# Squares for eight norms on ACT and their sums on DVE, in place of POOL, each behind the two parts of its tile

## The chip, the cores and the metric

The kernel runs on one core of one Trainium2 chip. The metric is device time in microseconds. The engines are named as the profile names them: PE (TensorE; PEld is its weight load), DVE (VectorE), ACT (ScalarE), POOL (GpSimd) and SP (SyncE, which issues nearly all transfers).

## What is computed

Two blocks in series on 256 tokens of width 1024, all in fp32. The first block has two layers: a gated feed-forward half step, then a state-space mixer (mamba) in layer 0 or a sliding-window attention in layer 1, then a second half step. The second block is a mixer of two parts (latent attention and a recurrence) and a retrieval feed-forward ("peer") of 16,384 experts. Each stage begins with a root-mean-square norm of the residual:

```python
def rmsnorm(x, g):
    xf = x.astype(jnp.float32)
    y = xf * lax.rsqrt(jnp.mean(xf * xf, axis=-1, keepdims=True) + EPS)
    return (y * g.astype(jnp.float32)).astype(x.dtype)

def swiglu_half_step(h, g, w1, w3, w2):
    u = rmsnorm(h, g)
    return h + FFN_HALF * ((jax.nn.silu(u @ w1) * (u @ w3)) @ w2)
```

There are eight such norms: one at the head of each of the four half steps, of the mamba mixer, of the attention, of the second block's mixer and of the peer stage.

## The kernel before

The residual `h` stays in on-chip memory, features on the partitions: eight tiles of 128 features by 256 tokens, `h[:, 0]` to `h[:, 7]`. Every fp32 product is made of three reduced-precision ones: an operand is split into a high part (rounded) and a low part (the rest), and `mm3` (lines 151 to 155) multiplies low by high, high by low and high by high into one sum. Weights come in chunks of eight blocks of 128 by 128 (`stream`, line 102): SP loads a chunk (`wraw`, four buffers), ACT rounds it (`whi`, line 93), DVE takes the difference (`wlo`, line 99); in the mixers some chunks have POOL take the difference.

The norm's factor is one number per token, so it is applied behind the first projection of a stage. What a stage needs first of the residual is therefore two things:

- The parts of `h` times the norm's gain. `split_x` (line 178) makes them tile by tile: ACT writes `xhi` (line 181), DVE writes `xlo` (line 182), which waits for it. In the peer stage they are called `uhi` and `ulo`.
- The sum of squares over the features. `norm_sum` (line 200) gives one tile's share at each step: on POOL a square (line 206 for tile 0, line 209 for the others, two buffers `sq`), and for tiles 1 to 7 an addition into `ssq` (line 210). `rs_tok` (line 184) then sums over the partitions with four small matmuls against ones (line 190), and DVE makes the reciprocal root in nine small steps (lines 168 to 176, tiles `qna`, `qny`, `qnt`, `rtn`). These matmuls stand behind the first one or two pairs of projections.

`norm_in` (line 213) runs both for seven norms: in each turn of its loop first the square and sum of tile k, then its split. The peer stage has the same loop written out, with the same order of square and split.

In a half step's second product the tiles of `h` come ready one after the other (line 319), some 8 us apart. Behind the mamba mixer (line 509), the attention and the second mixer (both line 261) they come in pairs: one addition of 512 columns finishes two tiles.

The program is written in one order, and a scheduler lays the instructions out on each engine's queue. On an engine they run strictly in that order.

Of the kernel before, what the change touches and what calls it, by code (L numbers as in the profile page):

```python
# [12 lines left out]
AF = mybir.ActivationFunctionType  # L13
# [5 lines left out]
KD = 8  # L19
# [29 lines left out]
class Ctx:  # L49
# [150 lines left out]
    def norm_sum(self, h):  # L200

        nc = self.nc
        acc = self.tmp.tile([128, T], F32, name="ssq", tag="ssq")
        for k in range(KD):
            if k == 0:
                nc.gpsimd.tensor_mul(acc, h[:, k], h[:, k])
            else:
                s = self.tmp.tile([128, T], F32, name="sq", tag="sq", bufs=2)
                nc.gpsimd.tensor_mul(s, h[:, k], h[:, k])
                nc.gpsimd.tensor_add(acc, acc, s)  # L210
            yield acc

    def norm_in(self, h, g):

        nc = self.nc
        hi = self.xp.tile([128, KD, T], F32R, name="xhi", tag="xhi")
        lo = self.xp.tile([128, KD, T], F32R, name="xlo", tag="xlo")
        for k, acc in enumerate(self.norm_sum(h)):
            self.split_x(h, g, hi, lo, k)

        def scale(between=None, tok=False):
            rt = self.rs_tok(acc, self.ones[:, 0:1], 1, 1.0 / 1024, EPS, "n")
            if tok:
                return rt
            if between is not None:
                between()
            ps = self.bank()
            for st in range(2):
                self.bcast(rt, st, 0, 128, ps[:, st * 128:(st + 1) * 128])
            rs = self.tmp.tile([128, T], F32, name="rs", tag="rs", bufs=2)  # L230
            nc.scalar.activation(rs, ps[:, :T], AF.Copy)
            return rs, rt

        return hi, lo, scale
# [1735 lines left out]
```

## Time and profile before

| what | us |
|---|---|
| three timed runs: lowest, median, highest | 2182.05, 2186.6, 2188.41 |
| profiled execution, its own time | 2188.62 |
| its span (first to last instruction) | 2186.8 |
| PE busy, share of the span | 2109.8, 96% |
| PEld busy | 1986.3, 91% |
| DVE busy | 1584.8, 72% |
| ACT busy | 1055.1, 48% |
| POOL busy | 407.1, 19% |

Busy matmul time is an upper bound of what PE needs, as matmuls overlap and their ends are modelled. What PE loses is to be read from its idle stretches and from the clock that it was granted, place by place. The mean granted clock of the profiled execution was 0.973 of full speed.

### The profile page before, as it was taken

The numbers are of one execution on the slowest core, as the hardware profiler recorded it, in microseconds if no ns is written. First come the engines' busy times: TensorE is split into PE (matmuls) and PEld (weight loads), VectorE is DVE, ScalarE is ACT, GpSimd is POOL, SyncE is SP. The second block draws the span as 40 slices with busy tenths as digits, with TensorE's granted clock in tenths as the row PEclk, the third lists the DMA queues.
The fourth block names the chain that finished last, engine by engine and source line by source line (L and its number), as shares of the span: only waits on it lengthen the run. The fifth ranks groups of instructions, "written<-read, shape, count | busy, mean of one in ns | idle before, by whom it ended". The sixth has DMA issues, their size and how long they took to land. (4 is left out here: it accounts for less than half of the span.)

```text
span 2186.8 us, 40880 instructions
## 1 busy us (share of the span) xinstructions
PE 2109.8 (96%) x16474; PEld 1986.3 (91%) x16474; DVE 1584.8 (72%) x2857; ACT 1055.1 (48%) x1770; POOL 407.1 (19%) x310
## 2 busy tenths in 40 slices
PE   8999898899999999999998998999999999999999
PEld 8999887799999998899997878999999998888887
DVE  7665979766567656676659678998788887555655
ACT  5444467444444445454443345553444444454454
POOL 2003335700110021100144315762000000000000
PEclk9999999999999999799998899999999999999999
DMA  6555442377555553245542205542444444555554
GB/s 218 190 185 177 136 135 101 134 191 204 185 181 184 183 184 107 102 169 188 188 164 76 80 30 194 177 151 97 157 162 155 159 160 164 189 188 191 192 188 150
DMA packets 98280, 348.14 MB, mean 159 GB/s; under 512 B 11083, under 2 KB 13996, under 8 KB 97836
## 3 DMA queue, kind: packets, MB, share of 16 engines
q1 hardware_dynamic: 98092, 345.54, 46.6%
q8 instruction: 129, 2.11, 0.4%
q14 instruction: 59, 0.48, 0.1%
HBM read 344.05 MB, written 1.44 MB: 158 GB/s over the span
## 5 line engine op out<-in xcount | busy, mean ns | idle before, releaser
L99 DVE TENSOR_TENSOR wlo<-wraw,whi 128x1024 fp32r<-128x1024 f32 x561 | 701.7, 1252 | 293.9 <-ACT whi L93 292.0
L93 ACT ACTIVATE whi<-wraw 128x1024 fp32r<-128x1024 f32 x644 | 676.5, 1053 | 394.0 <-PE ps L155 198.8
L153 PE MATMUL ps<-xhi,wlo 128*128 128x256 f32 x1960 | 562.7, 287 | 20.4 <-DVE wlo L99 9.6
L154 PE MATMUL ps<-xlo,whi 128*128 128x256 f32 x1960 | 557.3, 284 | 3.2 <-DVE xlo L182 2.6
L155 PE MATMUL ps<-xhi,whi 128*128 128x256 f32 x1960 | 554.9, 283 | 0.0
L153 PEld LDWEIGHTS ps<-xhi,wlo 128*128 128x128 f32 x1960 | 376.2, 192 | 28.8 <-DVE wlo L99 8.6
L154 PEld LDWEIGHTS ps<-xlo,whi 128*128 128x128 f32 x1960 | 376.1, 192 | 5.8 <-DVE xlo L182 5.4
L155 PEld LDWEIGHTS ps<-xhi,whi 128*128 128x128 f32 x1960 | 375.5, 192 | 0.2
L153 PE MATMUL ps<-phi,wlo 128*128 128x256 f32 x1024 | 293.9, 288 | 11.3 <-DVE wlo L99 4.6
L154 PE MATMUL ps<-plo,whi 128*128 128x256 f32 x1024 | 288.1, 281 | 0.0
L155 PE MATMUL ps<-phi,whi 128*128 128x256 f32 x1024 | 287.2, 281 | 0.0
L99 POOL TENSOR_TENSOR wlo<-wraw,whi 128x1024 fp32r<-128x1024 f32 (+1 forms) x83 | 206.8, 2495 | 167.5 <-ACT whi L93 145.5
L153 PEld LDWEIGHTS ps<-phi,wlo 128*128 128x128 f32 x1024 | 193.8, 190 | 13.1 <-DVE wlo L99 5.3
L1676 PE MATMUL pacc<-whi,cl 128*128 128x512 f32 x512 | 203.6, 398 | 1.5 <-DVE cl L1668 1.5
L1678 PE MATMUL pacc<-whi,ch 128*128 128x512 f32 x512 | 200.5, 392 | 0.0
L1677 PE MATMUL pacc<-wlo,ch 128*128 128x512 f32 x512 | 199.2, 389 | 0.0
L153 PE MATMUL ps<-ghi,wlo 128*128 128x256 f32 x704 | 197.9, 281 | 0.0
L154 PE MATMUL ps<-glo,whi 128*128 128x256 f32 x704 | 197.6, 281 | 0.0
L155 PE MATMUL ps<-ghi,whi 128*128 128x256 f32 x704 | 197.5, 280 | 0.0
L154 PEld LDWEIGHTS ps<-plo,whi 128*128 128x128 f32 x1024 | 194.0, 189 | 0.0
L155 PEld LDWEIGHTS ps<-phi,whi 128*128 128x128 f32 x1024 | 193.3, 189 | 0.0
L154 PEld LDWEIGHTS ps<-glo,whi 128*128 128x128 f32 x704 | 132.6, 188 | 0.0
(534 smaller groups left out, 3371.3 us busy)
## 6 DMA issues: line engine op xcount, KB each, us to landing
wraw<-in_w SPq DMA_DIRECT2D x262, 512.0 KB, 3.7
wraw<-in_p_u SPq DMA_DIRECT2D x128, 512.0 KB, 3.6
wraw<-in_p_v SPq DMA_DIRECT2D x128, 512.0 KB, 3.6
wraw<-in_m_win SPq DMA_DIRECT2D x40, 512.0 KB, 3.7
wraw<-in_x_win SPq DMA_DIRECT2D x20, 512.0 KB, 3.6
wraw<-in_m_wout SPq DMA_DIRECT2D x16, 512.0 KB, 3.7
wraw<-in_p_wpq SPq DMA_DIRECT2D x16, 512.0 KB, 4.3
wraw<-in_a_wq SPq DMA_DIRECT2D x8, 512.0 KB, 3.5
```

The costliest lines, as they stand in the source:

```text
L93: nc.scalar.activation(hi, w, AF.Copy)
L99: (nc.vector if lo_eng == "dve" else nc.gpsimd).tensor_sub(lo, w, hi.bitcast(F32))
L153: nc.tensor.matmul(ps, wl, xh, start=first, stop=False)
L154: nc.tensor.matmul(ps, wh, xl, start=False, stop=False)
L155: nc.tensor.matmul(ps, wh, xh, start=False, stop=last)
L1676: TE.matmul(o, cl[:, t], vh[:, f], start=False, stop=False)
L1677: TE.matmul(o, ch[:, t], vl[:, f], start=False, stop=False)
L1678: TE.matmul(o, ch[:, t], vh[:, f], start=False, stop=last)
```

## The change

```diff
--- before.py
+++ after.py
@@ -203,11 +203,11 @@
         acc = self.tmp.tile([128, T], F32, name="ssq", tag="ssq")
         for k in range(KD):
             if k == 0:
-                nc.gpsimd.tensor_mul(acc, h[:, k], h[:, k])
+                nc.scalar.activation(acc, h[:, k], AF.Square)
             else:
                 s = self.tmp.tile([128, T], F32, name="sq", tag="sq", bufs=2)
-                nc.gpsimd.tensor_mul(s, h[:, k], h[:, k])
-                nc.gpsimd.tensor_add(acc, acc, s)
+                nc.scalar.activation(s, h[:, k], AF.Square)
+                nc.vector.tensor_add(acc, acc, s)
             yield acc
 
     def norm_in(self, h, g):
@@ -215,8 +215,10 @@
         nc = self.nc
         hi = self.xp.tile([128, KD, T], F32R, name="xhi", tag="xhi")
         lo = self.xp.tile([128, KD, T], F32R, name="xlo", tag="xlo")
-        for k, acc in enumerate(self.norm_sum(h)):
+        sums = self.norm_sum(h)
+        for k in range(KD):
             self.split_x(h, g, hi, lo, k)
+            acc = next(sums)
 
         def scale(between=None, tok=False):
             rt = self.rs_tok(acc, self.ones[:, 0:1], 1, 1.0 / 1024, EPS, "n")
```

The square of a tile is taken by ACT and the addition by DVE. In `norm_in` the split of tile k now stands ahead of its square and sum; in the peer stage the square and sum still stand ahead of the split in the program's order. Lines behind 219 move by two: line 261 before is line 263 now.

How the queues change is shown at three places. The first is DVE behind the attention, at the last two pairs of tiles: `h<-h,ps` finishes a pair, `xlo` is the low part, `wlo` a chunk of the next half step's weights. Before:

```order
L99 TENSOR_TENSOR wlo<-wraw,whi 128x1024
L182 SCALAR_TENSOR_TENSOR xlo<-h,gains,xhi 128x256 x2
L261 TENSOR_TENSOR h<-h,ps 128x512
L99 TENSOR_TENSOR wlo<-wraw,whi 128x1024
L182 SCALAR_TENSOR_TENSOR xlo<-h,gains,xhi 128x256 x2
L99 TENSOR_TENSOR wlo<-wraw,whi 128x1024 x3
```

Now:

```order
L210 TENSOR_TENSOR ssq<-ssq,sq 128x256
L99 TENSOR_TENSOR wlo<-wraw,whi 128x1024
L182 SCALAR_TENSOR_TENSOR xlo<-h,gains,xhi 128x256
L263 TENSOR_TENSOR h<-h,ps 128x512
L210 TENSOR_TENSOR ssq<-ssq,sq 128x256
L182 SCALAR_TENSOR_TENSOR xlo<-h,gains,xhi 128x256
L210 TENSOR_TENSOR ssq<-ssq,sq 128x256
L182 SCALAR_TENSOR_TENSOR xlo<-h,gains,xhi 128x256
L210 TENSOR_TENSOR ssq<-ssq,sq 128x256
L182 SCALAR_TENSOR_TENSOR xlo<-h,gains,xhi 128x256
L210 TENSOR_TENSOR ssq<-ssq,sq 128x256
L99 TENSOR_TENSOR wlo<-wraw,whi 128x1024 x4
```

Each low part has an addition behind it, the pair's addition into `h` stands among them, and one `wlo` that stood ahead of the last two low parts stands behind them.

The second place is ACT at the very start; `whi` of 128x512 is half a chunk. Before:

```order
L181 ACTIVATE xhi<-h,gains 128x256 x2
L123 ACTIVATE whi<-wraw 128x512
L181 ACTIVATE xhi<-h,gains 128x256 x2
L123 ACTIVATE whi<-wraw 128x512
L181 ACTIVATE xhi<-h,gains 128x256 x4
L123 ACTIVATE whi<-wraw 128x512 x2
L93 ACTIVATE whi<-wraw 128x1024 x7
```

Now:

```order
L181 ACTIVATE xhi<-h,gains 128x256
L206 ACTIVATE ssq<-h 128x256
L181 ACTIVATE xhi<-h,gains 128x256
L123 ACTIVATE whi<-wraw 128x512
L209 ACTIVATE sq<-h 128x256
L181 ACTIVATE xhi<-h,gains 128x256
L209 ACTIVATE sq<-h 128x256
L123 ACTIVATE whi<-wraw 128x512
L181 ACTIVATE xhi<-h,gains 128x256
L209 ACTIVATE sq<-h 128x256
L181 ACTIVATE xhi<-h,gains 128x256
L209 ACTIVATE sq<-h 128x256
```

Squares stand between the high parts, and seven of the eight stand ahead of the last high part.

The third place is ACT at the peer stage's norm; `bhi` belongs to the mixer, `pq` to the peer's first product. Before:

```order
L1417 ACTIVATE ahi<-ps,px 128x128 x8
L93 ACTIVATE whi<-wraw 128x1024 x2
L1187 ACTIVATE bhi<-ps 128x4x128
L93 ACTIVATE whi<-wraw 128x1024 x5
L181 ACTIVATE uhi<-h,pa 128x256 x8
L93 ACTIVATE whi<-wraw 128x1024
L1542 ACTIVATE pq<-ps 128x256
```

Now:

```order
L206 ACTIVATE ssq<-h 128x256
L209 ACTIVATE sq<-h 128x256
L93 ACTIVATE whi<-wraw 128x1024
L209 ACTIVATE sq<-h 128x256 x2
L93 ACTIVATE whi<-wraw 128x1024
L209 ACTIVATE sq<-h 128x256 x2
L181 ACTIVATE uhi<-h,pa 128x256 x6
L209 ACTIVATE sq<-h 128x256
L181 ACTIVATE uhi<-h,pa 128x256
L209 ACTIVATE sq<-h 128x256
L181 ACTIVATE uhi<-h,pa 128x256
L93 ACTIVATE whi<-wraw 128x1024
```

Six squares stand ahead of all high parts, beside the chunks that still belong to the mixer's last product; two stand ahead of the last two high parts.

On PE the order changes at five places by a few matmuls. At two of them, behind mamba and behind the attention, four matmuls that before stood among the first projection's, with a later weight chunk, now stand behind it. At the attention's norm the four small matmuls on `ssq` move behind the first projection. On POOL the 120 instructions of lines 206, 209 and 210 go, and no other is added.

## Rows read from the trace of the kernel before

**Rows 1.** The page, part 1: busy time, share of the span, instructions.

```profile
PE 2109.8 (96%) x16474; PEld 1986.3 (91%) x16474; DVE 1584.8 (72%) x2857; ACT 1055.1 (48%) x1770; POOL 407.1 (19%) x310
```

**Rows 2.** Groups by line, POOL: count | busy us, mean ns | idle before.

```profile
L210 POOL TENSOR_TENSOR ssq<-ssq,sq 128x256 f32<-128x256 f32 x56 | 58.5, 1045 | 3.3
L209 POOL TENSOR_TENSOR sq<-h 128x256 f32<-128x256 f32 x56 | 52.2, 939 | 159.6 <-DVE h L319 152.3 <-DVE nsink L657 5.5 <-DVE h L261 1.0
```

**Rows 3.** Line 182 by itself: min/median/max ns, first and last start.

```profile
L182 DVE SCALAR_TENSOR_TENSOR xlo<-h,gains,xhi x56: 472/831/2620, 4.8 to 1120.5; 128x256 fp32r<-128x256 f32 x56
L182 DVE SCALAR_TENSOR_TENSOR kvlo<-h,gains,kvhi x8: 472/475/476, 629.3 to 633.2; 128x256 fp32r<-128x256 f32 x8
```

**Rows 4.** Groups by line, DVE and ACT: busy us, mean ns of 128x256 operations.

```profile
L289 DVE TENSOR_TENSOR glo<-fab,ghi 128x256 fp32r<-128x256 f32 x88 | 37.2, 424 | 31.8 <-ACT ghi L288 31.8
L182 DVE SCALAR_TENSOR_TENSOR ulo<-h,pa,uhi 128x256 fp32r<-128x256 f32 x8 | 6.1, 832 | 0.0
L286 ACT ACTIVATE fab<-fab 128x256 f32<-128x256 f32 x88 | 35.4, 402 | 9.5 <-DVE fab L284 9.5
```

**Rows 5.** Timeline, DVE, attention to the next block: start us, us, what.

```profile
919.23 1.37 DVE L99 TENSOR_TENSOR wlo<-wraw,whi 128x1024 fp32r<-128x1024 f32 x1 [0.40 <-ACT whi L93]
...
928.76 0.68 DVE L261 TENSOR_TENSOR h<-h,ps 128x512 f32<-128x512 f32 x1
...
931.00 1.70 DVE L182 SCALAR_TENSOR_TENSOR xlo<-h,gains,xhi 128x256 fp32r<-128x256 f32 x2
```

**Rows 6.** Timeline, POOL, the same place.

```profile
929.28 2.39 POOL L210 TENSOR_TENSOR ssq<-ssq,sq 128x256 f32<-128x256 f32 x2
```

**Rows 7.** Timeline, PE, the same place.

```profile
926.36 0.28 PE L155 MATMUL ps<-ohi,whi 128*128 128x256 f32 x1
...
930.03 0.38 PE L153 MATMUL ps<-xhi,wlo 128*128 128x256 f32 x1 [0.64 <-ACT xhi L181]
```

**Rows 8.** Busy time by stretch: PE, PEld, DVE, ACT, POOL (x), PEclk, DMA, GB/s.

```profile
13.80:22.60 8.80, 8.78 (x73) 8.67 (x74) 7.36 (x7) 3.18 (x3) 6.63 (x5) 1.00 0.66 216
933.00:943.00 10.00, 10.00 (x75) 10.00 (x74) 3.68 (x3) 3.35 (x4) 1.59 (x3) 0.83 0.48 165
```

**Rows 9.** Timeline, DVE, mixer (mamba) to the next block.

```profile
425.62 3.30 DVE L182 SCALAR_TENSOR_TENSOR xlo<-h,gains,xhi 128x256 fp32r<-128x256 f32 x2 [0.86 <-ACT xhi L181]
...
429.44 1.21 DVE L99 TENSOR_TENSOR wlo<-wraw,whi 128x1024 fp32r<-128x1024 f32 x1
...
435.44 0.68 DVE L509 TENSOR_TENSOR h<-h,wo 128x512 f32<-128x512 f32 x1
...
437.74 1.70 DVE L182 SCALAR_TENSOR_TENSOR xlo<-h,gains,xhi 128x256 fp32r<-128x256 f32 x2
```

**Rows 10.** Timeline, POOL, the same place.

```profile
426.04 2.59 POOL L99 TENSOR_TENSOR wlo<-wraw,whi 128x1024 fp32r<-128x1024 f32 x1
```

**Rows 11.** Timeline, DVE, last block to the router (peer).

```profile
1335.78 6.11 DVE L182 SCALAR_TENSOR_TENSOR ulo<-h,pa,uhi 128x256 fp32r<-128x256 f32 x8
```

**Rows 12.** Timeline, PE, first waiting matmul at four other norms.

```profile
203.29 0.31 PE L154 MATMUL ps<-xlo,whi 128*32 128x256 f32 x1 [0.72 <-DVE xlo L182]
...
629.45 0.39 PE L154 MATMUL ps<-xlo,whi 128*128 128x256 f32 x1 [0.38 <-DVE xlo L182]
...
829.08 0.61 PE L190 MATMUL ps<-ones,ssq 128*128 128x1 f32 x4 [0.41 <-POOL ssq L210]
...
1125.25 0.61 PE L190 MATMUL ps<-ones,ssq 128*128 128x1 f32 x4 [0.61 <-POOL ssq L210]
```

**Rows 13.** Timeline, ACT, the first microseconds.

```profile
7.90 0.63 ACT L123 ACTIVATE whi<-wraw 128x512 fp32r<-128x512 f32 x1 [0.98 <-DMA wraw<-in_w]
8.57 1.71 ACT L181 ACTIVATE xhi<-h,gains 128x256 fp32r<-128x256 f32 x4
```

**Rows 14.** Timeline, DVE, the first microseconds.

```profile
9.42 3.33 DVE L182 SCALAR_TENSOR_TENSOR xlo<-h,gains,xhi 128x256 fp32r<-128x256 f32 x4
```

**Rows 15.** Timeline, PE, the first microseconds.

```profile
13.82 0.38 PE L153 MATMUL ps<-xhi,wlo 128*128 128x256 f32 x1 [0.52 <-DVE wlo L124]
```

## The prediction

> **What bounds the kernel now.** I read the page first: PE is busy for 96% of the span [rows 1], so the work of the norms can only matter where PE waits for it. The two views that say where are the timeline of PE around each of the eight norms, and the timelines of DVE and POOL beside it. POOL is not the bound, and the 110.7 us that lines 209 and 210 take of it [rows 2] are not on PE's path as such. The question is what these POOL instructions do to DVE.
>
> A low part (line 182) lasts 472 to 475 ns where POOL is empty, which is the case for the eight `kvlo`, and in the median 831 ns beside POOL's squares [rows 3]. The longest took 2.62 us, and the pair that holds it ran 425.62 to 428.92 while POOL had a weight chunk from 426.04 to 428.63 [rows 9, 10]. So a DVE instruction with two tensors from on-chip memory waits until POOL's instruction ends, and the reverse: two POOL additions took 2.39 us beside a DVE chunk [rows 6], 1.2 us each, close to their mean of 1.05 us [rows 2]. The Trainium skill says the same of this pair of engines (SBUF — State Buffer, Who interferes with whom): whichever starts first holds a shared port for its whole instruction. The trace agrees, with the numbers above.
>
> This matters where DVE is behind. Behind the attention PE ended the last matmul of the residual at 926.64 [rows 7], but DVE added that pair into `h` only at 928.76, and ended the last low part at 932.70 [rows 5]. PE stood still in between [rows 7], and from 933 on it was granted 0.83 of full speed [rows 8]. Behind mamba the last low part ended at 439.44 [rows 9].
>
> **The change, part by part.** POOL loses 120 instructions, and its queue keeps only weight chunks near the norms. ACT gets 64 squares and DVE 56 additions. No row shows a square of this kind. The nearest is an activation of 128x256 from and to on-chip memory, 402 ns; the nearest to the addition is `glo`, 424 ns [rows 4]. DVE starts an instruction before the last one has ended: eight `ulo` of 832 ns fill 6.11 us, not 6.66 [rows 4, 11], an overlap of 0.08 us. ACT's high parts follow each other at 0.43 us (four in 1.71 us) [rows 13]. So from start to start I take 0.34 us for an addition, 0.40 for a low part alone, 0.40 for a square, 1.13 for a chunk (1.21) [rows 9] and 0.60 for a pair's addition into `h` (0.68) [rows 5].
>
> *The middle tiles of the half steps* come some 8 us apart and meet a DVE and an ACT that wait for PE there; 0.34 and 0.40 us per tile cost nothing. If that cover were gone, the first to be late would be a weight chunk, with buffers for three ahead.
>
> *Four norms at which one tile is last.* PE waited 0.72 us (mamba) and 0.38 us (third half step) for the last low part, and 0.41 us (attention) and 0.61 us (second mixer) for POOL's sum [rows 12]. Alone the low part is 0.36 us shorter, and the chunk ahead of it at mamba isn't stretched either: I take 0.6 and 0.35 us back. At the second mixer the sum is on DVE, ahead of a chunk: 0.6 us. At the attention PE's order now has the low part first, which is just late: 0.2 us. Together 1.75 us (between 1.2 and the whole 2.1).
>
> *Behind the attention.* From 919.23 [rows 5] DVE has, up to the last low part, three chunks instead of four (the order shows the fourth behind), eight low parts, three pairs, and six additions: 3.4 + 3.2 + 1.8 + 2.0 = 10.4 us. With some 0.4 us of waits for ACT the last low part ends at 930.0 instead of 932.70. PE had used 0.5 us of its wait for four matmuls of a later sum, which it can't any more. That leaves 2.2 us. The ends are 1.5 us, if ACT's squares delay the high parts, and 3.8 us, if the lower clock behind it goes as well.
>
> *Behind mamba.* The first two low parts wait for POOL's chunk as before. From 429.44 [rows 9] on there are two chunks instead of three ahead of the last low part, six low parts, two pairs, and five additions: 2.3 + 2.4 + 1.2 + 1.7 = 7.6 us, which gives 437.05 instead of 439.44. Six matmuls that PE then did early (0.12 us each: 73 in 8.78 us [rows 8]) come off: 1.6 us (between 1.0 and 3.2, as above). If POOL merely slowed DVE, as the median of 831 against 475 ns could also be read, the first two low parts would not block, and it would be 2.7 us. By the skill's rule of the held port they do block; with it the whole sum is 6.3 us, without it 7.4. I go by the rows of the blocked pair, which are the nearer ones [rows 9, 10].
>
> *The peer stage.* Eight low parts follow each other, 6.11 us [rows 11]; now eight at 0.40 and two additions, 3.9 us: 2.2 us (between 1.5 and 2.6, for two squares of 0.40 us ahead of the last high parts, and for the chunks ahead of them that POOL no longer stretches).
>
> *The very start costs.* DVE was slowed here too (four low parts in 3.33 us [rows 14]), but ACT now has seven squares ahead of the last high part, and DVE additions between the low parts. From 7.90, where ACT gets the second half chunk [rows 13], it has five high parts, three half chunks and four squares up to the last high part: 2.1 + 1.6 + 1.6 = 5.3 us, so 13.2, where all high parts were done at 10.28 [rows 13]. The last low part then ends near 14.2, and the second half of the first projection starts near 14.45 instead of 13.82 [rows 15]: +0.6 us. PE also idles more in these microseconds. If it is then at the lower of its two levels, 1.2 instead of 2.4 GHz, those 24 matmuls cost another 24 x 0.12 = 2.9 us. I take +1.5, between +0.6 and +3.5, nearer to the lower end, since the clock is free to rise within them.
>
> **The sum.** +1.5 - 1.75 - 2.2 - 1.6 - 2.2 = -6.25, so 6.3 us less. Against the profiled execution's 2188.62 that is 2182.3. That execution lies 2.0 us above the median of the runs, 2186.6; the forecast for the median is **2180.3 us**. With all bounds at one end the gain is 11.1 us (2175.5), at the other 1.7 us (2184.9).
>
> **Rivals.** *The clock comes back.* Behind the attention PE lost 0.17 of 10 us to the lower level [rows 8]. With shorter waits both this stretch and the like one behind mamba may stay at the higher level: 3.2 us more, 2177.1. For it: the waits there shrink by half. Against it: PE still waits for low parts five to seven, one by one.
>
> *The start stays slow.* PE runs the whole second half of its first projection at the lower level: 3.5 instead of 1.5 us lost, 2182.3. For it: PE will have long gaps between 8 and 14 us. Against it: before, it was also idle in part there, and ran at full speed by 13.8 [rows 8]. The Trainium skill has a rule for this (TensorE: Matmul & The Clock Gate, What's actually happening): the slow level is the default, and activity releases it. By that rule this rival is what would happen, as the gaps now lie where the activity was; the granted clock at the start is what will tell.
>
> *Slower.* POOL is not what lengthens the low parts, so they stay at 0.83 us, and every addition is work put in front: seven at the start (2.4 us), five behind mamba (1.7), six behind the attention (2.0), two and two squares at the peer stage (1.5), less 0.8 us of waits for POOL's sum: 6.8 us more, 2193.4. The place is the DVE queue behind the attention. It decides by one duration: a low part and its addition together have to stay under the 0.83 us of a low part now, so the low part alone under 0.83 - 0.34 = 0.49 us; above that the queue is longer than before. Against it: `kvlo` on the same engine between the same neighbours at 475 ns [rows 3].
>
> **How the numbers follow.** I give the forecast 0.55, the clock's return 0.17, the slow start 0.22, and the slower case 0.06. A difference of 0.3%, about what a measurement can tell here, is 6.6 us, and the forecast's 6.3 lies almost on it: of its 0.55 I count 0.26 as over and 0.29 as within. So faster by over 0.3% is 0.26 + 0.17 = 0.43; within it 0.29 + 0.22 = 0.51; slower 0.06. The first three cases with their bounds reach from 2175.5 to 2184.9; the runs before lie up to 4.5 us from their median, so I take 1.5 us more below and 2.6 above. The range, 2174.0 to 2187.5, leaves out the last case.
>
> **What would show it.** In the changed profile the median of line 182 should be near 475 ns, with the longest still over 2 us behind mamba. Behind the attention the last low part should end about 2.7 us sooner after the same matmul, and behind mamba 2.4. The four small waits should be gone or under 0.2 us. At the start the second half of the first projection should begin 0.6 us later, and the granted clock there tells the first two cases of the start apart. Squares should take 0.40 us and additions 0.42. The forecast is wrong if low parts stay over 0.7 us, if a chunk on ACT is late because of squares in front of it during the half steps' second products, or if the total differs although these places move as said; then a place that I take to be unchanged has moved.

## The result and the profile after

The changed kernel takes 2175.54 us in the median of 18 runs (2163.42 to 2179.73), the kernel before 2185.41 in the median of 18 (2173.3 to 2195.81). The ratio is **0.9947, 95% interval 0.9929 to 0.9965**: 0.53% faster (0.35 to 0.71), in microseconds 0.0053 x 2185.4 = 11.6 (7.7 to 15.5). The two medians lie 9.9 us apart. The forecast was 6.3 us, and the likeliest single outcome in it was a difference within 0.3%. The time lies in the range that was given, 1.5 us above its lower end. The profiled execution took 2176.04 us, 12.6 less than that of before.

On the page of the changed kernel POOL's share falls (19% before, [rows 1]), and PE's rises by one point, which is the smaller span:

```profile
PE 2105.8 (97%) x16474; PEld 1983.6 (91%) x16474; DVE 1581.8 (73%) x2913; ACT 1074.8 (49%) x1834; POOL 292.8 (13%) x190
```

DVE has 56 instructions more and is busy for 3 us less. Line 182 by itself says why (min/median/max ns; compare [rows 3]):

```profile
L182 DVE SCALAR_TENSOR_TENSOR xlo<-h,gains,xhi x56: 470/479/2334, 4.9 to 1112.9; 128x256 fp32r<-128x256 f32 x56
L182 DVE SCALAR_TENSOR_TENSOR kvlo<-h,gains,kvhi x8: 477/479/481, 629.4 to 633.4; 128x256 fp32r<-128x256 f32 x8
L182 DVE SCALAR_TENSOR_TENSOR ulo<-h,pa,uhi x8: 475/476/478, 1325.4 to 1328.8; 128x256 fp32r<-128x256 f32 x8
```

The median went from 831 to 479 ns, the value that `kvlo` always had. The longest is still 2.33 us. Squares and additions cost what the nearest rows said (groups by line, ACT and DVE: busy us, mean ns):

```profile
L209 ACT ACTIVATE sq<-h 128x256 f32<-128x256 f32 x56 | 22.3, 402 | 0.5 <-DVE ssq L210 0.4
L210 DVE TENSOR_TENSOR ssq<-ssq,sq 128x256 f32<-128x256 f32 x56 | 23.4, 418 | 0.2
```

Behind the attention (timeline of DVE, the changed kernel; compare [rows 5]), the last low part now ends at 926.35, which is 11.6 us after the first of these `h` additions has begun at 914.75:

```profile
914.75 0.69 DVE L263 TENSOR_TENSOR h<-h,ps 128x512 f32<-128x512 f32 x1 [0.52 <-PE ps L155]
...
923.47 0.68 DVE L263 TENSOR_TENSOR h<-h,ps 128x512 f32<-128x512 f32 x1
...
925.87 0.48 DVE L182 SCALAR_TENSOR_TENSOR xlo<-h,gains,xhi 128x256 fp32r<-128x256 f32 x1
926.26 0.42 DVE L210 TENSOR_TENSOR ssq<-ssq,sq 128x256 f32<-128x256 f32 x1
```

In the kernel before, the additions at the same places began at 424.07 behind mamba and at 918.14 behind the attention (timeline of DVE):

```profile
424.07 0.69 DVE L509 TENSOR_TENSOR h<-h,wo 128x512 f32<-128x512 f32 x1 [7.64 <-PE wo L155]
...
918.14 0.69 DVE L261 TENSOR_TENSOR h<-h,ps 128x512 f32<-128x512 f32 x1 [0.67 <-PE ps L155]
```

The last low part behind the attention ended at 932.70, 14.6 us later. So DVE is 3.0 us sooner here (2.7 was forecast). Behind mamba (compare [rows 9]) the same distance is now 439.94 + 0.47 - 427.69 = 12.7 us, where it was 439.44 - 424.07 = 15.4: 2.7 us sooner (2.4 forecast).

```profile
427.69 0.69 DVE L511 TENSOR_TENSOR h<-h,wo 128x512 f32<-128x512 f32 x1 [7.67 <-PE wo L155]
429.23 2.73 DVE L182 SCALAR_TENSOR_TENSOR xlo<-h,gains,xhi 128x256 fp32r<-128x256 f32 x2 [0.85 <-ACT xhi L181]
...
439.94 0.47 DVE L182 SCALAR_TENSOR_TENSOR xlo<-h,gains,xhi 128x256 fp32r<-128x256 f32 x1
```

The pair of 2.73 us is the one that still meets a weight chunk on POOL, as forecast. What the forecast had only as a rival stands in the next rows: the ten microseconds behind both last low parts (busy time by stretch; after the POOL column PEclk, DMA share, GB/s), where [rows 8] had a granted clock of 0.83 behind the attention, and where the first row here, of the kernel before, has 0.91 behind mamba; the two below it are the changed kernel's:

```profile
439.50:449.50 10.00, 10.00 (x80) 10.00 (x80) 3.92 (x5) 3.80 (x4) 1.82 (x3) 0.91 0.47 147
```

```profile
440.50:450.50 10.00, 10.00 (x88) 10.00 (x89) 5.95 (x12) 4.24 (x4) 0.00 (x0) 1.00 0.67 194
926.40:936.40 10.00, 10.00 (x87) 10.00 (x88) 5.89 (x9) 4.24 (x4) 0.00 (x0) 1.00 0.57 179
```

PE now runs at its full clock through both.

What PE waited for just before these stretches in the kernel before were low parts, and weight chunks (`wlo`) in the same DVE queue (timeline of PE, behind mamba and then behind the attention):

```profile
434.82 0.39 PE L154 MATMUL ps<-xlo,whi 128*128 128x256 f32 x1 [1.08 <-DVE xlo L182]
...
437.97 0.55 PE L153 MATMUL ps<-xhi,wlo 128*128 128x256 f32 x1 [0.88 <-DVE wlo L99]
...
931.23 0.36 PE L153 MATMUL ps<-xhi,wlo 128*128 128x256 f32 x1 [0.81 <-DVE wlo L99]
```

At each of the two places there was a wait for a high part besides (0.63 us, and 0.64 in [rows 7]). These two places, behind mamba and behind the attention, are called the handovers from here on.

**Where the time went, place by place.** Each matmul of one program has its like in the other (same source line, same operands, same count). The table takes the difference of their start times, in the median over a stretch behind a place less the median over a stretch ahead of it. All columns are against the first profile of the kernel before; `again` and `third` are further executions of the same two kernels, described below. The first eight rows are the places of the eight norms, in the order of the program; negative is sooner.

```
us                      before  before   after   after   after
                        again   third    first   again   third
start of the program      2.25    1.37    2.56    1.89    2.36
mamba's norm             -0.01    0.00   -0.66   -0.66   -0.66
behind mamba              0.09   -0.01   -3.33   -2.74   -2.99
third half step           0.00    0.00   -0.48   -0.48   -0.49
attention's norm         -0.01    0.00   -0.20   -0.20   -0.20
behind the attention      0.01    0.24   -4.35   -3.57   -4.35
second mixer's norm       0.00    0.01   -0.88   -0.88   -0.88
peer stage's norm         0.01    0.14   -2.30   -1.97   -1.99
inside mamba              1.95    1.15    1.71    2.35    1.66
inside the attention      0.06    0.02   -2.99   -0.01   -2.99
inside the second mixer  -4.41   -4.02   -1.95   -3.93   -1.68
```

The seven norms behind the start repeat to within 0.8 us, four of them to 0.01. They sum to -12.2, -10.5 and -11.6 us, -11.4 in the mean, which is the size of the measured 11.6. The start, the first row, is taken up below. Inside the mixers the *same* program differs by several us between executions.

### The profile page after: what moved, and what is told of

It is laid out like the page before. It is cut to its first block, busy times and chain, and to the rows that moved or that the text cites. A ratio compares the mean times of both kernels' runs of the same rounds, so it can differ in the third digit from the quotient of the medians.

```text
span 2174.2 us, 40862 instructions
## 1 busy us (share of the span) xinstructions
PE 2105.8 (97%) x16474; PEld 1983.6 (91%) x16474; DVE 1581.8 (73%) x2913; ACT 1074.8 (49%) x1834; POOL 292.8 (13%) x190
```

## The experiments

**The change, cut into pieces.** A list of norms says which ones follow the change; the others keep the code of before.

```diff
+        if i in ACT_NORMS:
+            self.split_x(h, g, hi, lo, k)
+            acc = next(sums)
+        else:
+            acc = next(sums)
+            self.split_x(h, g, hi, lo, k)
```

Not shown: `norm_sum` picks its engines by the same list, in the peer stage too.

*All but the first norm:*

> The first norm as in the kernel before (squares and sums on POOL, ahead of the split), the other seven as changed. If the first norm costs what the trace shows (matmuls at 214 ns each until 18.25 us instead of 11.38), this is 2.5 us faster than the changed kernel: ratio to before about 0.9936, the first projection ends as in the kernel before (sum's first matmul near 22.6 instead of 25.1), and nothing else moves. If the 2.5 us would be caught up behind the first stage (transfers set the pace there), the ratio stays at 0.9947.

Measured 0.9937 (0.9911 to 0.9963). The first sum's matmul came at 25.55 us, not 22.6, though the start was that of the kernel before. The first clause of the expectation failed, which is what led to the repeats below. Its ratio, 0.9936, was met by luck: the sum came 2.95 us later than that clause has it, and the interval covers 0.9947 as well.

*Only the two norms behind mamba and behind the attention:*

> Only the norms behind mamba and behind the attention changed. If both handovers gain the wait and the clock that was lower behind it, as the trace says, 3.2 + 4.0 = 7.2 us less: ratio 0.9967, and full granted clock behind both. If the waits alone were the cause and the clock's return was chance, 3.8 us as forecast: 0.9983, with the clock down behind one or both.

Measured 0.9957 (0.9932 to 0.9982). By place: -3.0 behind mamba, -3.5 behind the attention, nothing at the other norms (0.5 at most). The interval covers the first expectation and just misses the second; the places decide. The clock behind both was full:

```profile
440.50:450.50 10.00, 9.90 (x82) 9.70 (x83) 5.83 (x8) 3.50 (x4) 0.00 (x0) 1.00 0.73 203
929.00:939.00 10.00, 9.77 (x79) 9.37 (x80) 6.44 (x9) 3.83 (x5) 0.00 (x0) 1.00 0.60 201
```

*The other five:*

> The norms of mamba, third half step, attention, second mixer and peer stage changed; start and handovers as before. By the places in the trace 0.65 + 0.6 + 0.5 + 0.9 + 2.1 = 4.7 us less: ratio 0.9978. If the further 3 us that the changed kernel gained inside the attention and the second mixer also come from the change, 7.9 us less: 0.9964.

Measured 0.9969 (0.9946 to 0.9992), which covers both expectations; by place -0.65, -0.48, -0.20, -0.88 and -2.2, and at the two handovers nothing, with the clock down behind both, as before (the ten microseconds behind the last low part):

```profile
444.70:454.70 10.00, 10.00 (x79) 10.00 (x79) 3.90 (x5) 3.77 (x4) 1.87 (x3) 0.91 0.55 150
934.30:944.30 10.00, 9.95 (x72) 9.95 (x72) 3.76 (x3) 3.18 (x3) 1.90 (x3) 0.83 0.47 160
```

*Only the first norm:*

> Only the first norm changed. By the trace 2.5 us slower: ratio 1.0011, the sum's first matmul near 25.1 us. If the start is caught up later, 1.000.

Measured 1.0003 (0.9973 to 1.0033), first sum's matmul at 24.22 us. The interval covers both expectations.

**The same two kernels again**, unchanged, one execution each:

> The kernel before, unchanged, profiled once more. If the later start of the other profiles with the old first norm (first sum's matmul at 25.4 to 25.7 us, where the first profile had 22.6) is the execution's and not the program's, this one lies anywhere between 22.5 and 26, and the stretches inside the mixers differ from the first profile by some us each, while the seven norms do not (by less than 0.3 us each). If the first profile was the rule for the old start, 22.6.

> The changed kernel, unchanged, profiled once more. If the start is the execution's, the first sum's matmul comes anywhere between 22.5 and 26 us; if the new first norm costs 2.5 us, near 25.1. The seven other norms as in its first profile: -0.7, -3.3, -0.5, -0.2, -4.4, -0.9, -2.3 us against before, within 0.3 each.

> As before_again: a third execution of the kernel before. Start between 22.5 and 26 us if it is the execution's, 22.6 if it is the program's; the norms as in the first profile.

> As after_again: a third execution of the changed kernel. Start between 22.5 and 26 us if it is the execution's, 25.1 if it is the program's; the norms as in its first profile.

They took 2188.81, 2178.78, 2187.99 and 2176.19 us. The first sum's matmuls, in this order (timeline of PE, one row of each of the four kernels, then the first execution of the changed one):

```profile
24.83 0.50 PE L190 MATMUL ps<-ones,ssq 128*128 128x1 f32 x4
```

```profile
24.46 0.50 PE L190 MATMUL ps<-ones,ssq 128*128 128x1 f32 x4
```

```profile
23.94 0.50 PE L190 MATMUL ps<-ones,ssq 128*128 128x1 f32 x4
```

```profile
24.94 0.50 PE L190 MATMUL ps<-ones,ssq 128*128 128x1 f32 x4
```

```profile
25.14 0.50 PE L190 MATMUL ps<-ones,ssq 128*128 128x1 f32 x4
```

With the old first norm there are now six executions: 22.58, 24.83 and 23.94 in the kernel before, and 25.55, 25.38 and 25.74 in the three kernels above that keep it; mean 24.7. With the new one four: 25.14, 24.46 and 24.94 in the changed kernel, and 24.22; mean 24.7. The start of the first profile of before was the earliest of its kind. Of the two kernels alone the means are 23.8 and 24.8 us. The three kernels that keep the old norm are not quite its like: the third high part starts at 7.6 us in them, against 6.0 to 6.8 in the kernel before. So what the new start costs lies between nothing and some 1 us, and these runs don't settle it.

Four of the seven other norms repeat to 0.01 us in the changed kernel. The other three differ from its first profile by more than the 0.3 us that was expected: by up to 0.8 behind the attention, 0.6 behind mamba and just over 0.3 at the peer stage.

**What it is in POOL.** The changed kernel, and POOL does dead work per tile of the residual, into a tile that nobody reads (shown for tiles 1 to 7; tile 0 has a square alone):

```diff
+            nc.gpsimd.tensor_mul(self.dacc, h[:, k], h[:, k])
+            nc.gpsimd.tensor_add(self.dacc, self.dacc, self.dacc)
```

> The changed kernel, and on top of it POOL takes a square and an addition of 128x256 per tile as before, into a tile that nobody reads. If POOL's instructions are what stretches DVE's, low parts go back to a median near 0.83 us and additions to near 0.8, both handovers lose their gain of 3.2 and 4.0 us and more, as DVE's queue now holds the additions too: ratio 0.998 to 1.004. If the gain came from the order of the queues or from the sums being ready sooner, nothing reads the POOL tile and the ratio stays at 0.9947.

Measured **1.0052** (1.0029 to 1.0075): the gain is gone and as much lost on top. The low parts are long again (first row, line 182), the additions at 641 ns in the mean instead of 418 (second, groups by line), and behind mamba PE waits for low parts (timeline, the row with the longest wait):

```profile
L182 DVE SCALAR_TENSOR_TENSOR xlo<-h,gains,xhi x56: 471/828/2548, 4.8 to 1132.0; 128x256 fp32r<-128x256 f32 x56
```

```profile
L210 DVE TENSOR_TENSOR ssq<-ssq,sq 128x256 f32<-128x256 f32 x56 | 35.9, 641 | 0.2
```

```profile
444.82 0.38 PE L154 MATMUL ps<-xlo,whi 128*128 128x256 f32 x1 [2.43 <-DVE xlo L182]
```

By place: +3.3 behind mamba, +2.1 behind the attention, +1.6 at the peer stage. Nothing reads what POOL made, and the traces have the instructions of DVE, ACT and PE in the same order as in the changed kernel, one by one; so neither the order of the queues nor sums that are ready sooner can be the cause by themselves.

Next, two copies, and two fills with zeros, in place of the dead square and addition. Tile 0 gets one copy in the first kernel, and a square in the second. In both the order on DVE, ACT and PE is again that of the changed kernel.

```diff
+            nc.gpsimd.tensor_copy(self.dacc, h[:, k])
+            nc.gpsimd.tensor_copy(self.dacc, h[:, k])
```

> The changed kernel, and POOL makes two copies of 128x256 per tile into a tile that nobody reads, in place of the dead square and addition. If any POOL instruction that reads on-chip memory stretches DVE's low parts, their median is 0.7 us or more and the handovers lose their gain (each +2 us or more against the changed kernel). If only instructions with two input tensors do, the median stays at 0.48 us and the handovers keep -3 and -4 us.

```diff
+            nc.gpsimd.tensor_copy(self.dacc[:, :1], h[:, k, :1])
+            nc.gpsimd.memset(self.dacc, 0.0)
+            nc.gpsimd.memset(self.dacc, 0.0)
```

> As dead_pool_copies, but POOL fills the tile with zeros twice (one element of the tile of the residual is copied first, so that it comes at the same time). If POOL being busy is enough, low parts are long and the handovers lose their gain; if it takes a read (or two), low parts stay at 0.48 us and the handovers keep -3 and -4 us, the ratio 0.9947.

Measured 0.9991 (0.9962 to 1.002) with copies, 0.9913 (0.9876 to 0.9951; only five runs, not told apart from 0.9947) with fills. Line 182, with copies and then with fills:

```profile
L182 DVE SCALAR_TENSOR_TENSOR xlo<-h,gains,xhi x56: 471/612/2339, 4.8 to 1118.3; 128x256 fp32r<-128x256 f32 x56
```

```profile
L182 DVE SCALAR_TENSOR_TENSOR xlo<-h,gains,xhi x56: 467/478/2496, 5.0 to 1118.9; 128x256 fp32r<-128x256 f32 x56
```

A copy reads one tensor and that is enough: 612 ns, under the "0.7 or more" that was expected. A copy is shorter than a square (519 and 662 ns in the mean against 939 [rows 2]), which may be why. The places: +1.2 behind mamba, -0.9 behind the attention. A fill reads nothing (the one element and the squares of tile 0 apart) and leaves the median where it was: 478 ns, and -2.6 and -3.9 at the handovers. At the peer stage only 0.6 of the 2.1 us is left, as the lower clock there costs 5.1 us in this execution, and 3.4 in the three of the changed kernel. The Trainium skill (SBUF — State Buffer, Who interferes with whom) has a DVE instruction with two inputs from on-chip memory contend with POOL instructions that read it and not with those that only write; these three runs agree.

**Half of the change each.** `nc.vector.tensor_add` back to POOL, squares on ACT; then the squares back to POOL, additions on DVE:

```diff
-                nc.vector.tensor_add(acc, acc, s)
+                nc.gpsimd.tensor_add(acc, acc, s)
```

> Squares on ACT, additions still on POOL: half of POOL's instructions remain and DVE gets none. If POOL's instructions stretch DVE's one by one, fewer low parts are long (median 0.5 to 0.8 us); the handovers win perhaps half of the 7.2 us, the waits for POOL's sum at the attention and the second mixer shrink: ratio 0.996 to 0.998. If it were POOL being busy at all, ratio near 1.000; if POOL's squares alone did it, 0.9947 or less.

```diff
-                nc.scalar.activation(s, h[:, k], AF.Square)
+                nc.gpsimd.tensor_mul(s, h[:, k], h[:, k])
```

> Squares still on POOL, additions on DVE: the other half. POOL's squares stretch DVE, and DVE's additions wait for them ahead of the next low parts: worse than the other half, ratio 0.998 to 1.003. If the number of POOL's instructions alone counts, the same as the other half.

Measured 0.9984 (0.9962 to 1.0006) and 1.004 (1.0012 to 1.0068). In the first, the median of the low parts is 948 ns, longer than expected; nothing is gained behind mamba (0.0), 2.1 us behind the attention, where the clock stayed full, and 2.2 at the peer stage. In the second DVE stands in front of POOL's square (timeline of DVE behind mamba):

```profile
428.23 2.61 DVE L210 TENSOR_TENSOR ssq<-ssq,sq 128x256 f32<-128x256 f32 x1 [1.37 <-POOL sq L209]
```

By place this half loses 1.8 us behind mamba, 3.3 at the second mixer's norm and 2.1 at the peer stage. So the first half keeps less than half of the gain and is not told apart from no change; the second, moving the sums alone, is worse than not moving anything.

**The order, and the price of the added work.** Sums behind all eight splits (the peer stage too); then, on the new engines, the old order in the loop; then no squares but the first (the norm's factor comes from one tile of eight):

```diff
         for k in range(KD):
             self.split_x(h, g, hi, lo, k)
+        for k in range(KD):
             acc = next(sums)
```

> The changed kernel with the squares and sums written behind all eight splits (peer stage too): behind the handovers two or three additions less stand ahead of the last low parts, at the peer stage no square ahead of the last high parts. If what PE still waits for there is these (0.33 + 0.71 + 0.11 us behind mamba, 0.23 behind the attention), 0.8 + 0.2 us less there and some 0.5 at the peer stage: 1.5 us, ratio 0.9940. If the sum is then late for its small matmuls, a wait of the same size there and 0.9947.

Measured 0.9924 (0.9894 to 0.9953), which is not told apart from 0.9947. At the handovers nothing came of the 1.0 us that was expected (-3.25 and -4.34). A new wait took the place: the scheduler now lays a weight chunk ahead of the last two low parts, and PE waits for that (timeline of PE behind mamba):

```profile
435.93 0.39 PE L153 MATMUL ps<-xhi,wlo 128*128 128x256 f32 x1 [0.64 <-ACT xhi L181]
436.95 0.36 PE L153 MATMUL ps<-xhi,wlo 128*128 128x256 f32 x1 [0.64 <-DVE wlo L99]
```

against these of the changed kernel, 1.28 us against 1.04 there:

```profile
437.67 0.39 PE L154 MATMUL ps<-xlo,whi 128*128 128x256 f32 x1 [0.33 <-DVE xlo L182]
...
439.00 0.38 PE L154 MATMUL ps<-xlo,whi 128*128 128x256 f32 x1 [0.71 <-DVE xlo L182]
```

The start was early in this execution: the first sum's matmul came at 22.04 us, earlier than in any of the ten above. Two squares stand ahead of the last high part there, and seven in the changed kernel.

```diff
         for k in range(KD):
-            self.split_x(h, g, hi, lo, k)
             acc = next(sums)
+            self.split_x(h, g, hi, lo, k)
```

> The changed kernel with the old order in the loop: square and sum of a tile ahead of its split, on the new engines. ACT's high part then waits 0.4 us for the square, DVE's additions stand ahead of the low parts: if the order matters, each of the four norms with one last tile and both handovers lose some 0.4 to 0.8 us: 4 us, ratio 0.9965. If engines alone matter, 0.9947.

Measured 0.9941 (0.9914 to 0.9967): the total doesn't tell the two apart. The places do in part: the order costs nothing at the four norms with one last tile (0.1 us each at most), 0.4 behind the attention, but behind mamba only 0.9 of the 3.0 us is left. PE waits there for one low part, 0.95 us, and the clock falls behind it:

```profile
438.99 0.38 PE L154 MATMUL ps<-xlo,whi 128*128 128x256 f32 x1 [0.95 <-DVE xlo L182]
```

```profile
440.00:450.00 10.00, 9.78 (x67) 9.37 (x67) 4.79 (x7) 3.32 (x4) 0.00 (x0) 0.83 0.51 157
```

> The changed kernel without the squares and additions of tiles 1 to 7 (the norm's factor then comes from one tile in eight): the added work taken out. If the additions ahead of the last low parts are what PE still waits for, 1.15 us behind mamba, 0.2 behind the attention and 0.8 at the peer stage come off: 2.2 us more than the changed kernel, ratio 0.9937. If weight chunks then end last, under 0.7 us: 0.9944 or more.

Measured 0.9914 (0.988 to 0.9947). By place against the mean of the changed kernel: 1.2 us more behind mamba, 0.7 behind the attention, 0.5 at the attention's norm, 2.2 at the peer stage, 4.5 in all, twice what was expected. The start was the earliest of all, with the first sum's matmul at 20.91 us. So the added squares and additions do cost, and what they cost is less than what POOL's did.

## Why the prediction was right in its mechanism and wrong in its size

**The mechanism** is as predicted, and shown by taking it away and putting it back: POOL's reads stretch DVE's two-input instructions (831 to 479, and 828 ns with dead work), and DVE's queue at the two handovers is what PE waits for. Behind mamba the new order has a part in it: with the old one 2.1 of the 3.0 us are lost again. The landmarks hold: the median of line 182, the longest still over 2 us, the last low parts 3.0 and 2.7 us sooner (2.7 and 2.4 forecast), squares at 402 and additions at 418 ns. Of the four small waits one is left, 0.22 us at the attention's norm. One reading in the prediction is wrong, though its sum goes by DVE's queue and not by that: behind the attention PE did not stand still from 926.64 on. It went on with the first projection's matmuls, and in the 6.4 us from 926.6 it was busy for 4.61.

**The terms**, against the mean of three executions:

| term | forecast | measured |
|---|---|---|
| very start | +1.5 | not settled: 0 to +1.1 |
| four norms | -1.75 | -2.2 (0.66 + 0.48 + 0.20 + 0.88) |
| behind mamba | -1.6 | -3.0 |
| behind the attention | -2.2 | -4.1 |
| peer stage | -2.2 | -2.1 |
| sum | -6.25 | -11.4, without the start |

**The step that failed: the clock at the handovers.** The forecast priced the waits there, -1.6 and -2.2, and left the lower clock behind them in place, as a bound and a rival with a chance of 0.17. The lower clock cost 1.7 us at each place: in all five profiles with the old handovers (three of before, the five other norms, the first norm alone) 1.7 us are lost to the clock behind either (each stretch of 4 us, times what the granted clock there lacks of 1), and in the five profiles that have both handovers as changed (three of after, the first norm on POOL, the handovers alone) none. The measured 3.0 and 4.1 less 1.7 are 1.3 and 2.4: the waits had been sized about rightly, and the clock came back each time, where the forecast gave it one chance in six. The reason that the forecast gave against it, PE still waits for low parts five to seven, is true behind mamba (0.33 and 0.71 us) and didn't decide. What PE did there doesn't give a rule. Behind mamba it waited 1.08, 0.63 and 0.88 us before, and the clock fell; now it waits 0.33 and 0.71, and the clock held. With the sums behind all splits it waited 0.64 twice and the clock held; with the old order in the loop it waited once for 0.95, and the clock fell. The Trainium skill (TensorE: Matmul & The Clock Gate, What's actually happening) has activity as what releases the throttle. That PE with shorter waits keeps the higher level agrees; no run here shows where the bound lies.

**The second, not settled: the start.** The +1.5 was priced from one execution, whose start happened to be the earliest of six. The part of it that is a delay is there: the second half of the first projection begins at 15.26, 14.45 and 15.12 us in the three executions of the changed kernel, against 13.82, 14.18 and 13.89, in the mean 1.0 us later where 0.6 was forecast. The part that is the clock was no difference between the kernels: in the changed kernel the first projection runs at the lower of the two levels far longer, 0.21 us from matmul to matmul until 18.25 us and 0.12 from there on,

```profile
18.03 0.41 PE L154 MATMUL ps<-xlo,whi 128*128 128x256 f32 x1
18.25 0.34 PE L155 MATMUL ps<-xhi,whi 128*128 128x256 f32 x1
18.43 0.28 PE L153 MATMUL ps<-xhi,wlo 128*128 128x256 f32 x1
```

but the same lasts until 18.8 and 17.2 us in the two other executions of the kernel before, against 11.4 in the first. The second part of the residual arrives at any time between 6.0 and 7.7 us in these profiles (the third high part starts then), and the clock's rise moves with the execution. So the rival of the slow start came largely true in both kernels, and tells them apart by little. That squares and additions ahead of the last parts do cost there is what the two earliest starts suggest (sums behind all splits, and one square, one execution each): their second half began at 12.36 and 11.92 us, although the second part of the residual came late, at 7.2 and 7.5 us.

**The third, small: the second mixer's norm,** -0.88 instead of -0.6; the other three of the four were forecast at -1.15 and came to -1.34.

With the clock put right the forecast's own sum is -6.25 - 3.4 = -9.7 us, and with a start that costs nothing -11.2; the measured interval, 7.7 to 15.5 us less, holds both. The prediction's last sign of being wrong, a place taken to be unchanged that has moved, is what came true: the stretches behind the handovers. The chances came from the sum: at 6.3 us it lay on the bound of 0.3%, so "within 0.3%" got 0.51, and the time fell under it.

**Open.** Inside the attention the changed kernel is 3.0 us sooner in two of three executions and not at all in the third; the granted clock from 838 to 905 us is 0.77, 0.72 and 0.77 in these, and 0.72 or 0.73 in all three of before. The five other norms alone have the 3.0 us (0.77), all but the first norm don't (0.72). Whether the shift of 0.2 to 0.9 us ahead of it tilts this or chance does, no run here tells.

## What to carry to other kernels

Where an engine's small work delays another through a shared resource, ask for the price at each place where the slower queue is the one waited for, and put the clock behind it in the sum: if the profile shows the granted clock down behind a wait, price its return as a term of its own. Here it came back in every profile that had the whole change at these places, and not behind mamba with the old order in the loop. Before a term of one or two microseconds is read from a stretch of one execution, read the same stretch in a second one; the start and the mixers here differ by 2 to 4 us with nothing changed. And move a chain of work whole: half of this one moved was not told apart from nothing, or cost time.

## What the runs showed of the hardware

- The time of one and the same program spreads over 1% (2173.3 to 2195.81 us for the kernel before), mostly in stretches where PE has gaps of its own. The largest seen: inside the attention the granted clock was 0.72 or 0.73 in all three profiles of the kernel before, and 0.95 in two of the experiments' (squares on POOL with sums on DVE, and the old order in the loop), which were 12.6 and 12.4 us sooner there. One stretch without gaps differs too: in most of the fourth half step matmuls come 0.113 us apart in three profiles (the handovers alone, POOL's copies, and squares on POOL with sums on DVE) and 0.118 in the other fifteen, with a granted clock of 1.00 in both, which is 3.6 us. Nothing here shows why.
- At the very start the profile's granted clock reads 1.00 while the matmuls run at the lower of the two levels (0.21 against 0.12 us apart). The level is better read from the distance of matmuls there.
- A POOL copy with one input stretches a DVE instruction with two (612 ns in the median against 479), a fill doesn't (478).
